# Spreading the output-weight splits of a paged-attention stage over more pages, and ordering three groups of casts

## The chip, the core and the metric

The kernel runs on one core of a Trainium2 chip. Its time is the device time of one execution, in microseconds (us). The profiled execution is one more execution, recorded by the hardware profiler.

## The reference

Two layers of a hybrid decoder: a Mamba-2 SSD layer and a multi-head latent attention (MLA) layer, on a prompt of 1024 tokens and on 8 samples of 8 new tokens with 2048 cached positions each. Everything is float32. The part of the reference that the change touches:

```python
def mla_prompt_attn(q_nope, q_pe, ckv, kpe, w_uk, w_uv):     # per block of 128 queries
    _, l, acc = latent_partial(absorb(qn, w_uk), qp, ckv, kpe, q_pos[:, None] >= k_pos[None, :])
    return latent_out(l, acc, w_uv)

def mla_sample_attn(q_nope, q_pe, ckv, kpe, pool_ckv, pool_kpe, layer, page_table, w_uk, w_uv):
    q_lat = absorb(q_nope, w_uk)
    stats = latent_partial(q_lat, q_pe, ckv, kpe, causal)          # the sample's own 8 keys
    def page_step(carry, pt):                                      # 16 pages of 128 keys
        page = latent_partial(q_lat, q_pe, pool_ckv[layer, pt], pool_kpe[layer, pt], None)
        return merge_partial(carry, page), None                    # running maximum, sum, values
    (_, l, acc), _ = lax.scan(page_step, stats, page_table.T)
    return latent_out(l, acc, w_uv)

def mla_output(o, gate, w_out):                                    # for prompt and samples
    gated = o.reshape(b, t, MLA_WIDTH) * jax.nn.silu(gate)
    return jnp.einsum('bte,ed->btd', gated, w_out)                 # 1024 x 1024
```

After that come the residual and a final RMSNorm.

## The kernel before

**Precision.** A float32 product is made as three matmuls on rounded operands: each operand is split into a high part and a low part (`hi` and `lo`), and hi·hi, hi·lo and lo·hi are summed. A split is two instructions: ScalarE (ACT) copies the source into `hi`, rounding it, and then VectorE (DVE) or GpSimd (POOL) subtracts: `lo = src - hi`. The helper `split` (lines 125 to 133) issues both; its argument `parts` cuts the subtraction into that many instructions.

**Stages.** The SSD layer ends at about 1060 us, the MLA projections at about 1335 us. Then come the prompt's sixteen heads (to about 1680 us), and the *pages stage* (from about 1680 us to about 1926 us), and a short tail.

**Heads.** `mla_heads` writes the order on TensorE (PE) and GpSimd by hand. Beside the attention of head h, units of preparation for head h+2 are merged in. For every fourth head `prep_group` (lines 1239 to 1271) loads the key weights (`wkr`, line 1245) and value weights, splits both, and makes eight value pieces (`vp`, written to `Vh` and `Vl`); the key weights (`w` in the trace) are used after the eighth piece, by `prep_kv`. The split of the key weights stands behind piece i = 3 in the text. The order of ACT, DVE and the DMA queue of SyncE (SP) is made by a planner that simulates the kernel: it may move an instruction ahead of the ones written before it, as soon as its inputs are there in the simulation. `issue_after(x)` restrains it: an instruction in that block that runs on x's own engine is placed behind x. On instructions of another engine it has no effect.

**Pages.** `Sample.flow` (lines 1777 to 1824) goes over 32 items, four for each sample, each of 4 x 128 keys; I call item n "page n". In the iteration n the hand-written PE order is: first half of the transposes of page n+1 (`turn(n+1, 0)`), transposes of the weights of page n-1 (`turn_p(n-1)`), the second half (`turn(n+1, 1)`), on every fourth page the transposes of a finished sample (`turn_acc`), scores of page n, a block of output matmuls (`next(out.fill)`), and values of page n-1. DVE and ACT make of that: `cTh`, `cTl` (turned page, high and low), `pTh`, `pTl` (turned weights), the maximum `mx` and its running negative `nm` (`softmax`, line 1635), the exponentials `P`, and the accumulator `ac`. GpSimd gathers page n+4 (`pgr`) and makes the low half `kvl` of page n+1 (`halves`).

**Output weights.** The eight blocks of 128 rows of `w_out`, in the order `WORD`, are split in the iterations that `WSP` lists: two each in pages 2, 3, 4 and 5. `weight_split` (lines 1867 to 1879) issues the copy `w5h` on ACT behind the turned page's `cTh` and four subtractions of 256 columns (`w5l`), on GpSimd for the first, third, fifth and seventh block, on DVE for the others (`WENG`), the latter behind `cTl`. Blocks 2 to 7 go through three load buffers (`w5r`) that the rows `h` of the output use later; the first two blocks have their own (`w5p`).

**Output rows.** `pieces` (lines 1881 to 1951) is a generator over eight tiles of 128 prompt rows. Its first step loads a tile (`og`), the second splits it (`oh` on ACT, `ol` as one DVE instruction of 1024 columns), and each further step issues 12 of a tile's 48 output matmuls (`p`). The flow takes the splitting step in page 5 (`OUT0[0] - 1`), one step in pages 6 and 7 (`OUT0`) and in every page after that, and a second one in pages 8 and 12 (`MORE`).

Of the kernel before, what the change touches and what calls it, by code (L numbers as in the profile page):

```python
# [8 lines left out]
F32 = mybir.dt.float32  # L9
F32R = mybir.dt.float32r  # L10
AF = mybir.ActivationFunctionType
ALU = mybir.AluOpType
# [25 lines left out]
SCALE = (NOPE + ROPE) ** -0.5  # L38
# [9 lines left out]
QG = 2  # L48
PRE = 4
Q0 = 9  # L50
OUT0 = (6, 7)
MORE = (8, 12)
WSP = (2, 2, 3, 3, 4, 4, 5, 5)
WENG = (2, 0, 2, 0, 2, 0, 2, 0)
WORD = (0, 4, 6, 1, 2, 3, 5, 7)
NWA = 8
# [26 lines left out]
def mm3(nc, out, pairs):  # L83
    n = len(pairs)
    for i, (a, b) in enumerate(pairs):
        nc.tensor.matmul(out, a, b, start=(i == 0), stop=(i == n - 1))  # L86
# [38 lines left out]
def split(k, hi, lo, src, eng=None, parts=0):  # L125
    nc = k.nc
    nc.scalar.copy(hi, src)  # L127
    n = parts and hi.shape[1] // parts
    for a in range(parts):
        s = slice(a * n, a * n + n)  # L130
        (eng or nc.vector).tensor_tensor(lo[:, s], src[:, s], hi[:, s].bitcast(F32), op=ALU.subtract)
    if not parts:
        return (eng or nc.vector).tensor_tensor(lo, src, hi.bitcast(F32), op=ALU.subtract)  # L133
# [1013 lines left out]
class Heads:  # L1147
# [91 lines left out]
    def prep_group(self, hg):  # L1239
        k, nc = self.k, self.k.nc  # L1240
        cs = slice(256 * hg, 256 * hg + 256)
        w8 = self.w8
        self.wkr = w8[0]
        self.wk = w8[2 + 2 * (hg % 2)], w8[3 + 2 * (hg % 2)]
        nc.sync.dma_start(self.wkr, self.wuk[:, cs].rearrange("(k p) e -> p k e", p=128))
        raw, wv = w8[1], w8[6:]
        nc.sync.dma_start(raw, self.wuv[:, cs].rearrange("(k p) e -> p k e", p=128))
        yield
        split(k, *wv, raw)
        if hg == 1:  # L1250
            self.ones_cols(1)
        yield
        vh, vl = self.V[hg % 2]
        for i in range(8):
            t0 = 128 * i
            p = self.wt(f"vp{hg}{i}")
            pairs = []
            for kk in range(2):
                a, b = k.kvh[:, kk, t0 : t0 + 128], k.kvl[:, kk, t0 : t0 + 128]
                pairs += [(a, wv[0][:, kk]), (a, wv[1][:, kk]), (b, wv[0][:, kk])]  # L1260
            mm3(nc, p[:, :256], pairs)
            src = p[:, :256].rearrange("p (a j v) -> p a j v", a=2, j=2)

            def dst(t):
                t = t[:, i]
                return bass.AP(t.tensor, t.offset, [list(t.ap[0]), [192, 2], [128, 2], [1, 64]])

            split(k, dst(vh), dst(vl), src)
            if i == 3:
                split(k, *self.wk, self.wkr)  # L1270
            yield

    def prep_kv(self, h):
# [265 lines left out]
class Sample:  # L1539
# [87 lines left out]
    def softmax(self, name, s, n, old):  # L1627
        nc = self.k.nc
        mx = self.small(name, "mx4", 1)
        nc.vector.reduce_max(mx, s, axis=AX.X)  # L1630
        nm = self.small(name, "nm4", 1, 4)
        if old is None:
            nc.vector.tensor_scalar(nm, mx, -SCALE, None, op0=ALU.mult)
        else:
            nc.vector.tensor_scalar(nm, mx, -SCALE, old, op0=ALU.mult, op1=ALU.min)
        P = self.sp.tile([128, n], F32, tag=f"P4{n}", name=f"P4{name}", bufs=2)
        l = self.small(name, "l4", 1, 4)
        nc.scalar.activation(P[:, :n], s, AF.Exp, bias=nm, scale=SCALE, accum_out=l)
        f = None
        if old is not None:  # L1640
            f = self.small(name, "f4", 1)
            nc.scalar.activation(f, old, AF.Exp, bias=nm, scale=-1.0)
        return nm, P, l, f
# [133 lines left out]
    def flow(self):  # L1777
        N = len(self.items)
        for n in range(-1, N + 1):
            t, out = n + 1 < N, self.out  # L1780
            if t:
                self.turn(n + 1, 0)
            if n % 4 == 1:
                self.first_acc(n // 4)
            if t:
                yield
            if n > 0:
                self.turn_p(n - 1)
            if t:
                self.turn(n + 1, 1)  # L1790
                yield
            if out:
                for x in range(WSP.count(n)):
                    out.weight_split(WORD[WSP.index(n) + x])
            if n % 4 == 1 and n > 4:
                self.turn_acc(n // 4 - 1)
            if 0 <= n < N:
                self.scores(n)
                self.weigh(n)
            if n % 4 == 3 and t:  # L1800
                self.first_scores(n // 4 + 1)
            if 0 <= n < N:
                yield
            if n % 4 == 0 and n < N:
                self.first_values(n // 4)
            if n >= 0 and n + PRE < N:
                self.load(n + PRE)
            if n == N - 2:
                self.late_loads()
            if n % 2 == 0 and n + 2 < N:  # L1810
                self.load_tk(n + 2)
            if out and (n in OUT0 or max(OUT0) < n <= N - HOLD):
                next(out.fill, None)
            if n > 0:
                self.values(n - 1)
            if t:
                self.halves(n + 1)
            if out:
                if n in MORE:
                    next(out.fill, None)  # L1820
                if n + 1 == OUT0[0]:
                    next(out.fill)
                    self.k.nc.sync.dma_start(out.fw, self.k.I["final_norm_w"].partition_broadcast(128))
            yield
# [27 lines left out]
class MlaOut:  # L1852
# [11 lines left out]
        self.raw[kk] = self.sp.tile([128, D], F32, tag="h5", name=f"w5r{kk}", bufs=3)  # L1864
        WQ(nc).dma_start(self.raw[kk], k.I["mla_w_out"][0][kk * 128 : kk * 128 + 128])

    def weight_split(self, kk):
        hi, lo = self.ws[kk]
        raw = self.raw.pop(kk)
        nc, x = self.k.nc, WENG[WORD.index(kk)]  # L1870
        with self.k.tc.issue_after(self.pins[0].ins):
            nc.scalar.copy(hi, raw)
        for a in range(4):
            s = slice(256 * a, 256 * a + 256)
            with self.k.tc.issue_after(self.pins[1].ins):
                (nc.gpsimd if x & 2 else nc.vector).tensor_tensor(lo[:, s], raw[:, s], hi[:, s].bitcast(F32),
                                                                  op=ALU.subtract)
        if 2 <= WORD.index(kk) < 5:
            self.weight(WORD[WORD.index(kk) + 3])

    def pieces(self, tiles, src=None):
        k, nc, sp, ws = self.k, self.k.nc, self.sp, self.ws

        def load(i):
            t0, m = TILES[i]
            oh = sp.tile([128, 8, 128], F32R, tag="oh5", name=f"oh5{i}", bufs=2)
            ol = sp.tile([128, 8, 128], F32R, tag="ol5", name=f"ol5{i}", bufs=2)
            g = src
            if i < 8:
                g = sp.tile([128, 8, 128], F32, tag="og5", name=f"og5{i}", bufs=2)  # L1890
                nc.sync.dma_start(g, k.og_d[:, :, t0 : t0 + m].rearrange("b p t -> p b t"))
            return oh[:, :, :m], oh[:, :, 64:] if m == 64 else ol, g, oh

        queue = [load(tiles[0])]
        if tiles[0] == 0:
            yield
        split(k, *queue[0][:3])
        if tiles[0] == 0:
            yield
        for n, i in enumerate(tiles):  # L1900
# [10 lines left out]
            for hf, c in enumerate(cs):  # L1911
                nw = c.stop - c.start
                tag = "tr" if src else "pj"
                p = self.psum.tile([128, 512], F32, tag=tag, name=f"p5{i}{hf}", bufs=SB[tag])
                for j, _ in enumerate(mm_tok(nc, p, m, nw, [
                        (oh[:, kk], ol[:, kk], o2[:, kk], ws[kk][0][:, c], ws[kk][1][:, c]) for kk in WORD])):
                    if j == (7 if src else 11) and nw == 512:
                        yield
                nc.vector.tensor_tensor(h[:m, c], h[:m, c], p[:m, :nw], op=ALU.add)
                if src:  # L1920
                    nc.vector.tensor_tensor(h[:m, c], h[:m, c], p[64:, :nw], op=ALU.add)
                    nc.scalar.activation(junk[:, c], h[:m, c], AF.Square, accum_out=ss[:m, hf : hf + 1])
                    if hf < 2:
                        nc.vector.tensor_tensor(h[:m, c], h[:m, c], self.fw[:m, c], op=ALU.mult)
                    if hf == 1:
                        nc.vector.tensor_tensor(ss[:m, 0:1], ss[:m, 0:1], ss[:m, 1:2], op=ALU.add)
                if hf == 0:
                    if n + 1 < len(tiles):
                        split(k, *queue[0][:3])
                if c.stop < D:  # L1930
                    yield
            if not src:
# [123 lines left out]
```

## Time and profile before

| | us |
|---|---|
| median of 3 runs | 1953.28 (1952.03 to 1955.74) |
| the profiled execution's own time | 1949.75 |
| its span, first to last instruction | 1948.0 |
| PE busy in the span | 1898.6 |
| DVE, ACT, POOL busy | 1189.8, 1108.4, 841.3 |

The profile is read from the page (totals, slices), then from views of the trace: busy time by stretch, waits by engine, and the instructions in order of time. In a row of the last kind stand the start, the time taken, the engine, the line in the kernel, the operation, output and input, and in brackets the idle time of that engine just before with what ended it.

### The profile page before, as it was taken

What the parts mean: (1) busy time and instruction counts of PE and PEld (TensorE: products, weight loads), DVE (VectorE), ACT (ScalarE), POOL (GpSimd) and SP (SyncE); (2) the same over time, 40 slices, a digit from 0 to 9 for tenths busy, and PEclk for the clock granted to TensorE, in tenths of its full rate; (3) what the DMA queues carried; (4) which work ended last, traced back from release to release, by engine and by line L of the source; (5) the groups of instructions that cost most, each with busy time, mean ns of one, the idle gap of its engine ahead of it and who ended that gap; (6) DMA issues with size and microseconds to landing.
All of it is one profiled execution on the core that took longest, in us unless ns stands there. A gap on an engine that the chain in (4) does not pass through costs nothing.

```text
span 1948.0 us, 33561 instructions
## 1 busy us (share of the span) xinstructions
PE 1898.6 (97%) x12023; PEld 1732.3 (89%) x12023; DVE 1189.8 (61%) x2423; ACT 1108.4 (57%) x2535; POOL 841.3 (43%) x1122
## 2 busy tenths in 40 slices
PE   9999999999999999899999999999999999899998
PEld 7999999999999999788788998898888888778887
DVE  5566565657666656755533104476787778666564
ACT  6466666667666666732214314336777777855552
POOL 2447455555655555443003212104443434865551
PEclk9999999999999999999999999999999999999999
DMA  5123223332323332544533333133111112654431
GB/s 167 48 72 93 86 85 97 84 108 84 96 81 96 86 95 82 190 161 156 181 114 117 123 150 94 56 109 94 48 49 41 51 40 59 215 181 149 144 128 38
DMA packets 181086, 202.01 MB, mean 104 GB/s; under 512 B 18828, under 2 KB 147608, under 8 KB 180536
## 3 DMA queue, kind: packets, MB, share of 16 engines
q1 hardware_dynamic: 175864, 180.08, 30.1%
q0 software_dynamic: 4976, 19.66, 2.9%
q8 instruction: 95, 1.56, 0.3%
q14 instruction: 71, 0.58, 0.1%
q10 hardware_dynamic: 80, 0.13, 0.0%
HBM read 146.52 MB, written 53.28 MB: 103 GB/s over the span
## 4 chain that ended last, share of the span: by engine, by line
PE 82%; ACT 5%; DMA 4%; DVE 4%; POOL 3%; issue 2%; SPq 0%; POOLq 0%; DVEq 0%; ACTq 0%
PE pj L86 19%; PE pz L98 8%; PE pq L98 6%; PE pob L98 5%; PE p L98 5%; PE poa L98 5%; PE sc L86 2%; PE py L635 2%; PE o L86 2%; DMA M<-acs_d 2%; PE o L1426 2%; PE sc L1363 2%; PE o L1428 2%; PE st L1395 2%; PE st L1397 2%
## 5 line engine op out<-in xcount | busy, mean ns | idle before, releaser
L86 PE MATMUL pj<-xh,wih 128*128 128x384 f32 (+1 forms) x768 | 254.2, 335 | 0.5 <-ACT raw L512 0.3
L86 PE MATMUL pj<-xl,wih 128*128 128x384 f32 (+1 forms) x768 | 253.7, 330 | 0.0
L86 PE MATMUL pj<-xh,wil 128*128 128x384 f32 (+1 forms) x768 | 253.2, 330 | 0.0
L1409 POOL TENSOR_TENSOR tl<-P,th 128x384 fp32r<-128x384 f32 (+1 forms) x96 | 91.3, 951 | 235.1 <-ACT P L1407 188.9
L526 DVE SCALAR_TENSOR_TENSOR acc<-raw,vec,acc 128x1112 f32<-128x1112 f32 x96 | 142.2, 1482 | 26.4 <-ACT acc L522 25.4
L86 PEld LDWEIGHTS pj<-xh,wih 128*128 128x128 f32 x768 | 143.9, 188 | 2.3 <-ACT xh L273 0.8
L86 PEld LDWEIGHTS pj<-xl,wih 128*128 128x128 f32 x768 | 144.5, 188 | 1.0
L86 PEld LDWEIGHTS pj<-xh,wil 128*128 128x128 f32 x768 | 144.4, 188 | 0.4
L98 PE MATMUL pz<-wih,xh 128*128 128x256 f32 x504 | 142.8, 287 | 0.6 <-ACT z L567 0.6
L98 PE MATMUL pz<-wil,xh 128*128 128x256 f32 (+1 forms) x504 | 140.2, 284 | 0.0
L1406 ACT ACTIVATE th<-st 128x512 fp32r<-128x512 f32 x192 | 94.5, 492 | 65.5 <-PE st L1402 50.5
L630 ACT ACTIVATE M<-M,tok 128x128 f32<-128x128 f32 (+1 forms) x288 | 90.9, 386 | 66.7 <-DVE M L627 66.3
L98 PE MATMUL pz<-wih,xl 128*128 128x256 f32 x448 | 128.3, 286 | 0.0
L1699 POOL TENSOR_TENSOR kvl<-pgr,kvh 128x256 fp32r<-128x256 f32 x128 | 96.3, 779 | 66.3 <-ACT kvh L1697 65.6
L98 PEld LDWEIGHTS pz<-wih,xh 128*128 128x128 f32 x504 | 95.9, 190 | 1.3 <-ACT z L567 1.0
L627 DVE TENSOR_TENSOR M<-M,negu 128x512 f32<-128x512 f32 x64 | 52.6, 822 | 68.3 <-DMA M<-acs_d 67.9
L1407 ACT ACTIVATE P<-st 128x512 f32<-128x512 f32 x192 | 93.7, 488 | 0.0
L98 PEld LDWEIGHTS pz<-wil,xh 128*128 128x128 f32 (+1 forms) x504 | 92.7, 184 | 0.7
L133 DVE TENSOR_TENSOR wil<-wraw,wih 128x512 fp32r<-128x512 f32 x88 | 71.3, 817 | 27.6 <-ACT wih L127 24.4
L613 POOL TENSOR_TENSOR xdd<-xsT,tok 128x256 f32<-128x256 f32 x64 | 50.8, 794 | 80.5 <-ACT xsT L599 80.1
L98 PEld LDWEIGHTS pz<-wih,xl 128*128 128x128 f32 x448 | 85.2, 190 | 0.1
L1409 DVE TENSOR_TENSOR tl<-P,th 128x512 fp32r<-128x512 f32 x96 | 70.9, 739 | 18.5 <-ACT P L1407 17.6
(832 smaller groups left out, 6302.7 us busy)
## 6 DMA issues: line engine op xcount, KB each, us to landing
wraw<-in_ssd_w_in SPq DMA_DIRECT2D x92, 256.0 KB
M<-acs_d SPq DMA_DIRECT2D x64, 256.0 KB
s<-in_state_ssm SPq DMA_DIRECT2D x32, 256.0 KB
y_d<-y SPq DMA_DIRECT2D x64, 128.0 KB
out_s_ssm<-s SPq DMA_DIRECT2D x32, 256.0 KB
wraw<-in_ssd_w_out SPq DMA_DIRECT2D x12, 512.0 KB
q_d<-qt SPq DMA_DIRECT2D x32, 192.0 KB
qp<-q_d SPq DMA_DIRECT2D x8, 768.0 KB
```

Source lines behind the costliest of these rows:

```text
L86: nc.tensor.matmul(out, a, b, start=(i == 0), stop=(i == n - 1))
L98: nc.tensor.matmul(o, a, b, start=(j == 0), stop=(j == len(ops) - 1))
L133: return (eng or nc.vector).tensor_tensor(lo, src, hi.bitcast(F32), op=ALU.subtract)
L526: last = nc.vector.scalar_tensor_tensor(acc, raw[:, j : j + n], k.convw[j][:, blk : blk + 1], acc, op0=ALU.mult, op1=ALU.add)
L613: nc.gpsimd.tensor_tensor(v3(xdd), v3(xsT), hb(2), op=ALU.mult)
L627: nc.vector.tensor_tensor(M[:m, :, :m], M[:m, :, :m], (k.negs if smp else k.negu)[:m, :m].unsqueeze(1).to_broadcast([m, 4, m]), op=ALU.add)
L630: nc.scalar.activation(M[:m, h, :m], M[:m, h, :m], AF.Exp, bias=tk[:, 0, 4 * g + h : 4 * g + h + 1])
L635: nc.tensor.matmul(py[:m, h * 64 : h * 64 + 64], M[:m, h, :m], xsT[:m, h * 64 : h * 64 + 64], start=True, stop=True)
L1406: nc.scalar.activation(th[:, :n], ps[:, :n], AF.Exp, scale=SCALE)
L1407: nc.scalar.activation(P[:, :n], ps[:, :n], AF.Exp, scale=SCALE)
L1409: eng.tensor_tensor(tl[:, :n], P[:, :n], th[:, :n].bitcast(F32), op=ALU.subtract)
L1699: nc.gpsimd.tensor_tensor(rl[:, j], raw[:, j], rh[:, j].bitcast(F32), op=ALU.subtract)
```

## The change

Four edits:

1. The eight blocks of the output weight are split in pages 2, 3, 4, 4, 5, 6, 6, 7. Each split is made in two halves: the copy and the first two subtractions are issued ahead of the page's scores (behind the turned page, as before), the other two behind the page's scores, and those on DVE behind the page's `nm`.
2. The steps of the output rows start two pages later (splitting in page 7, blocks in 8 and 9 and on), and the second steps are taken in pages 10, 12, 14 and 18. Their number up to page 32 is the same: 28 blocks.
3. `turn_acc` is issued behind the values of page n-1, no longer ahead of the scores. The subtraction `ol` of an output tile is made in four parts.
4. In `prep_group` the split of the key weights is placed behind the two instructions of the value piece i = 3.

```diff
-OUT0 = (6, 7)
-MORE = (8, 12)
-WSP = (2, 2, 3, 3, 4, 4, 5, 5)
+OUT0 = (8, 9)
+MORE = (10, 12, 14, 18)
+WSP = (2, 3, 4, 4, 5, 6, 6, 7)
@@ prep_group
-            split(k, dst(vh), dst(vl), src)
+            a = nc.scalar.copy(dst(vh), src)
+            b = nc.vector.tensor_tensor(dst(vl), src, dst(vh).bitcast(F32), op=ALU.subtract)
             if i == 3:
-                split(k, *self.wk, self.wkr)
+                with k.tc.issue_after(a.ins), k.tc.issue_after(b.ins):
+                    split(k, *self.wk, self.wkr)
@@ softmax
-            nc.vector.tensor_scalar(nm, mx, -SCALE, old, op0=ALU.mult, op1=ALU.min)
+            self.nmi = nc.vector.tensor_scalar(nm, mx, -SCALE, old, op0=ALU.mult, op1=ALU.min)
@@ flow
-            if out:
-                for x in range(WSP.count(n)):
-                    out.weight_split(WORD[WSP.index(n) + x])
-            if n % 4 == 1 and n > 4:
-                self.turn_acc(n // 4 - 1)
+            parts = [WORD[WSP.index(n) + x] for x in range(WSP.count(n))] if out else []
+            for kk in parts:
+                out.weight_split(kk, 0)
             if 0 <= n < N:
                 self.scores(n)
                 self.weigh(n)
+            if parts:
+                out.pins = out.pins[0], self.nmi
+            for kk in parts:
+                out.weight_split(kk, 1)
...
             if n > 0:
                 self.values(n - 1)
+            if n % 4 == 1 and n > 4:
+                self.turn_acc(n // 4 - 1)
@@ MlaOut
-    def weight_split(self, kk):
+    def weight_split(self, kk, half):
         hi, lo = self.ws[kk]
-        raw = self.raw.pop(kk)
+        raw = self.raw[kk]
         nc, x = self.k.nc, WENG[WORD.index(kk)]
-        with self.k.tc.issue_after(self.pins[0].ins):
-            nc.scalar.copy(hi, raw)
-        for a in range(4):
+        if not half:
+            with self.k.tc.issue_after(self.pins[0].ins):
+                nc.scalar.copy(hi, raw)
+        for a in range(2 * half, 2 * half + 2):
...
-        if 2 <= WORD.index(kk) < 5:
-            self.weight(WORD[WORD.index(kk) + 3])
+        if half:
+            del self.raw[kk]
+            if 2 <= WORD.index(kk) < 5:
+                self.weight(WORD[WORD.index(kk) + 3])
@@ pieces
-        split(k, *queue[0][:3])
+        split(k, *queue[0][:3], parts=4 if tiles[0] == 0 else 0)
...
-                        split(k, *queue[0][:3])
+                        split(k, *queue[0][:3], parts=4 if tiles[n + 1] < 8 else 0)
```

## The prediction, on record before the changed kernel was seen

> **What bounds the kernel now.** I read the totals first, then the waits of TensorE, then a table by stretch, then the instructions in order of time around the edits.
>
> ```profile
> PE 1898.6 (97%) x12023; PEld 1732.3 (89%) x12023; DVE 1189.8 (61%) x2423; ACT 1108.4 (57%) x2535; POOL 841.3 (43%) x1122
> PE 82%; ACT 5%; DMA 4%; DVE 4%; POOL 3%; issue 2%; SPq 0%; POOLq 0%; DVEq 0%; ACTq 0%
> ```
>
> PE is busy for 97% and carries 82% of the chain that ended last. The change removes no matmul, so it can only win where PE waits or runs slowly.
>
> ```profile
> PE o L86 <- DVE pTl L133: 5.4, 3, 2.4
> PE act L1757 <- DVE ac L1750: 2.7, 1, 2.7
> PE pt L1726 <- ACT P L1638: 0.9, 2, 0.5
> PE o L86 <- ACT pTh L127: 0.6, 1, 0.6
> 1682.00:1690.00 8.00, 6.88 (x45) 5.84 (x43) 5.71 (x10) 6.12 (x13) 5.33 (x7) 1.00 0.53 178
> 1690.00:1698.00 8.00, 5.57 (x30) 5.16 (x29) 8.00 (x18) 7.08 (x14) 7.81 (x10) 0.79 1.05 343
> 1698.00:1706.00 8.00, 4.49 (x30) 3.36 (x28) 7.49 (x9) 6.38 (x12) 7.81 (x10) 1.00 1.06 321
> 1706.00:1714.00 8.00, 5.71 (x25) 4.64 (x25) 7.45 (x14) 1.61 (x2) 7.72 (x10) 0.79 0.81 244
> 1714.00:1722.00 8.00, 7.74 (x49) 6.93 (x50) 4.89 (x12) 5.42 (x12) 4.91 (x6) 1.00 0.81 264
> 1722.00:1730.00 8.00, 8.00 (x53) 7.18 (x52) 4.56 (x12) 4.58 (x12) 3.85 (x5) 1.00 0.53 186
> ```
>
> The first four rows are PE's waits from 1681 to 1722 us (total, times, longest): 9.6 us. The others give busy time of PE, weight load, DVE, ACT and POOL in stretches of 8 us, then the granted clock. The five stretches to 1722 have 9.6 us of idle PE too, while DVE and POOL are full from 1690 to 1714; after 1722 PE is full. Twice the granted clock is 0.79: 2 x 0.21 x 8 = 3.4 us of work lost. So the split pages lose 13.0 us, and that is the ceiling of edits 1 and 3.
>
> What fills DVE there, in order of time:
>
> ```profile
> 1687.74 2.94 DVE L1876 TENSOR_TENSOR w5l<-w5p,w5h 128x256 fp32r<-128x256 f32 x4 [1.62 <-ACT w5h L1872]
> 1692.61 0.39 PE L86 MATMUL o<-kvh,pTl 128*128 128x256 f32 x1 [2.43 <-DVE pTl L133]
> 1701.17 4.64 DVE L133 TENSOR_TENSOR ol<-og,oh 128x1024 fp32r<-128x1024 f32 x1
> 1718.25 1.42 DVE L1876 TENSOR_TENSOR w5l<-w5r,w5h 128x256 fp32r<-128x256 f32 x4
> L1876 DVE TENSOR_TENSOR w5l<-w5r,w5h x12: 406/844/953, 1693.3 to 1719.2; 128x256 fp32r<-128x256 f32 x12
> L1876 POOL TENSOR_TENSOR w5l<-w5r,w5h x12: 716/813/1748, 1694.3 to 1713.2; 128x256 fp32r<-128x256 f32 x12
> ```
>
> A block's four subtractions stand ahead of the maximum and of `pTl`, and PE, which needs `pTl`, waits 2.43 us; a 1024-wide `ol` of 4.64 us stands ahead of `ac`, and `turn_acc` waits for that in front of the scores (the 2.7 us of the second wait row). A part on DVE takes 406 ns at best and 844 ns at the median; the four at 1718.25 took 1.42 us and those at 1687.74, beside POOL's own, 2.94.
>
> The last place is in the heads:
>
> ```profile
> 1446.80 0.62 ACT L127 CAST w<-w 128x512 fp32r<-128x512 f32 x1 [2.15 <-DMA w<-in_mla_w_uk]
> 1447.94 0.50 PE L1395 MATMUL st<-qTh,kTh 98*128 98x512 f32 x1 [1.49 <-ACT P L1407]
> 1535.94 0.62 ACT L127 CAST w<-w 128x512 fp32r<-128x512 f32 x1 [2.63 <-DMA w<-in_mla_w_uk]
> 1537.09 0.50 PE L1395 MATMUL st<-qTh,kTh 98*128 98x512 f32 x1 [1.95 <-ACT P L1407]
> L86 PE MATMUL vp<-w,kvh x28: 277/282/333, 1462.5 to 1473.5; 128*128 128x256 f32 x28
> ```
>
> The planner put the key weights' cast on ACT as soon as it believed their DMA landed; the chip's ACT waits 2.15 and 2.63 us for it, with the attention's exponentials behind it, and PE stands still for 1.49 and 1.95 us.
>
> **The change, part by part.**
>
> *Key weights (edit 4).* The cast moves behind piece 3 of the group. The pieces of the group loaded at 1442 run from 1462.5 us on (last row), 15 us after the early cast, so the DMA has landed. Removed: 1.49 + 1.95 = 3.4 us. Moved: 0.62 us on ACT and one subtraction on DVE, into a stage where PE is the bound; the cover is the two score tiles of lead, and if it is gone the cost is at most those 0.62 us twice, 1.2. I take 0: **-3.4**, bounds -3.4 and -2.2. Queued behind the pinned cast are the exponentials, as before, but without a wait in front.
>
> *Pages (edits 1 to 3).* I compare from the scores of page 2 to those of page 8:
>
> ```profile
> 1681.20 0.48 PE L86 MATMUL sc<-cTh,qlh 128*128 128x512 f32 x1
> 1686.54 0.48 PE L86 MATMUL sc<-cTh,qlh 128*128 128x512 f32 x1
> 1700.59 0.39 PE L86 MATMUL o<-kvh,pTl 128*128 128x256 f32 x1 [1.64 <-DVE pTl L133]
> 1707.11 0.78 PE L86 MATMUL sc<-cTh,qlh 128*128 128x512 f32 x1
> 1716.83 0.40 PE L98 MATMUL p<-w5h,oh 128*128 128x512 f32 x1
> 1719.58 0.28 PE L86 MATMUL o<-kvh,pTh 128*128 128x256 f32 x1
> 1730.07 0.48 PE L86 MATMUL sc<-cTh,qlh 128*128 128x512 f32 x1
> ```
>
> Now that is 1730.07 - 1681.20 = 48.9 us. It holds two output blocks of 2.75 us (1719.58 - 1716.83), in pages 6 and 7, that the change moves to pages 10 to 18, where PE is full and each costs its 2.75 us again. So these six pages must take under 48.9 - 5.5 = 43.4 us to win. PE's own work in them is 43.4 - 13.0 = 30.4, or 5.07 a page.
>
> What each page takes after the change:
> - Pages 2 and 5 have one block, on POOL. DVE has its ordinary work (the first four of these rows, over six pages): two `cTl`, `pTl`, the maximum, `nm`, `ac` and `ln`:
>
> ```profile
> L1688 DVE TENSOR_TENSOR cTl<-ct,cTh 128x512 fp32r<-128x512 f32 x12 | 8.2, 682 | 2.7 <-ACT cTh L1687 2.7
> L1630 DVE TENSOR_REDUCE mx<-sc 128x1 f32<-128x512 f32 x6 | 4.1, 681 | 0.5 <-PE sc L86 0.5
> L133 DVE TENSOR_TENSOR pTl<-pt,pTh 128x512 fp32r<-128x512 f32 x6 | 4.1, 680 | 0.0
> L1747 DVE SCALAR_TENSOR_TENSOR ac<-ac,f,o 128x256 f32<-128x256 f32 x6 | 2.9, 477 | 2.2 <-PE o L86 2.1
> L1699 POOL TENSOR_TENSOR kvl<-pgr,kvh 128x256 fp32r<-128x256 f32 x23 | 16.9, 763 | 3.2 <-ACT kvh L1697 2.8 <-issue 0.3
> L1619 POOL DMA_INDIRECT pgr<-in_cache_ckv,ptidx x6 | 6.3, 1042 | 1.5 <-POOL kvl L1699 0.9 <-POOL w5l L1876 0.5 <-DMA w5r<-in_mla_w_out 0.2
> L133 DVE TENSOR_TENSOR ol<-og,oh x8: 1210/1226/4641, 1696.9 to 1886.3; 128x1024 fp32r<-128x1024 f32 x8
> ```
>
>   (8.2 + 4.1 + 4.1 + 2.9)/6 = 3.2 us, and some 0.5 for `nm` and `ln` (an estimate from the smaller groups): 3.7. PE bounds these pages: 5.07 plus the wait for `P`, 0.5 (third wait row): 5.6.
> - Pages 3 and 7 have one block on DVE, pages 4 and 6 one on DVE and one on POOL. DVE then has 3.7 + 0.4 of small things + four parts: 3.0 beside a POOL split (the 2.94 row), 1.6 alone (4 x 406), so 7.1 in pages 4 and 6 and from 5.7 to 7.1 in pages 3 and 7, where POOL is busy for half the page; the middle is 6.4. The halves now stand behind `nm`, so the maximum no longer waits for four.
> - `ol` of the first tile, four parts of 256 columns, adds 1.6 to 3.4 us. DVE has 5.6 - 3.7 = 1.9 free in each of pages 2 and 5, and the planner fills gaps; I add 1.0.
>
> Sum: 2 x 5.6 + 2 x 7.1 + 2 x 6.4 + 1.0 = 39.2, against 43.4: **-4.2**. Bounds: all parts alone, 2 x 5.6 + 4 x 5.7 = 34.0, -9.4; all beside POOL and `ol` not hidden, 2 x 5.6 + 4 x 7.1 + 3.4 = 43.0, -0.4. No single wait in this is near 2.4 us, so I let the clock stay at 1.00, as after the 1.64 us wait at 1700.59 (the next stretch at 0.79 follows the wait for `ac`); that is inside the sum.
>
> POOL's own load is 4 blocks x 4 parts x 0.81 = 13 us, and six times (4 x 0.76 for `kvl` + 1.04 for the gather) = 24.5: 37.5 us in 39.2, nearly full but one page of slack ahead of PE. The second half of a POOL block isn't held by `nm`, which is on another engine; only its page changes. `turn_acc` behind the values costs nothing: it waits for `ac` of a page before, and its 0.4 us of PE work stays.
>
> The row that speaks against the DVE parts is 406/844/953: the same subtraction at twice the time. The Trainium skill, "GPSIMD Engine Reference", section "1. Specifications", says that GpSimd shares its SBUF interfaces with VectorE and that instructions with two SBUF inputs contend. By that rule alone every part pays while POOL runs, which is the upper bound above. The trace agrees as far as it goes: `w5l` and `ol`, with two such inputs, are stretched, `cTl` and `pTl`, which read PSUM, stay at 680 ns.
>
> *Later pages.* The double pages 12 and 18 begin a new half tile right behind a finished one, which waits for the addition of the finished one (page 12 and 18 by the count of blocks; before, page 12 alone):
>
> ```profile
> PE p L98 <- DVE h L1919: 0.6, 1, 0.6
> ```
>
> One more such wait: **+0.6**, from 0 to 0.6. The casts and subtractions of `ol` in four parts cost 8 x (4 x 0.41 - 1.22) = 3 us of DVE in all, against a free DVE (3.4 of 8 us in the stretch at 1722); PE hides it, and in a page without slack it would cost 0.4.
>
> **Sum.** -3.4 - 4.2 + 0.6 = -7.0 us. The profiled execution took 1949.75 us, 1.75 above its span; that would become 1942.8. It lies 3.5 us below the median, 1953.28, to which I apply the same difference: **1946.3 us**.
>
> **The rivals.**
> 1. *Slower: the split pages stay bound by DVE and POOL.* Pages 3 and 4 lasted from 1686.54 to 1707.11 (scores to scores), 10.3 us each, with both engines full. If pages 4 and 6, with two blocks, take 10.3 again (the planner, which doesn't know the slow parts, packs them ahead of `pTl`) and the four others 7.5, the six take 50.6: 7.2 over 43.4. With -3.4 and +0.6: +4.4, **1957.7**. It decides from 8.3 us a page on. For it: DVE at 8.00 of 8. Against it: the work is spread over six pages, and the chain scores, maximum, exponential gets ahead of half of it. 12%.
> 2. *The heads gain, the pages don't*: the work returns as smaller waits for `pTl`, `P` and `kvl`; 43.0 instead of 39.2, so -3.4 - 0.4 + 0.6 = -3.2: **1950.1**. It includes the case that the planner had these orders anyway. 12%.
> 3. *SP becomes the wait.* SP issues in order, and the late rows stand in front of the keys:
>
> ```profile
> 1711.98 8.08 SPq L1904 DMA_DIRECT2D h<-h_d  x3
> 1724.07 0.32 SPq L1612 DMA_DIRECT2D tk<-kpe_dh  x1
> ```
>
>    The three `h` loads take 8.08 us of queue, since their buffers come free with the last `w5l`. The last blocks are split later now; if those loads stand ahead of `tk` of page 8, its scores start late by about half a page, 3.5 us: -3.5, **1949.8**. Against it: today `tk` is issued at 1724.07, 6 us ahead of the scores of page 8. 10%.
> 4. *PE's floor is reached*: 34.0 and no second wait: -12.8, **1940.5**. 6%.
>
> **How the numbers follow.** My forecast has 60%, and its own bounds go from -3.4 - 9.4 to -2.2 - 0.4 + 0.6. The range holds rivals 2, 3 and 4 and half of rival 1: 1940.5 to 1955.0. A measurement of this kernel can tell about 0.2%, 3.9 us, from no change. Faster by more: the forecast but for its weak end, and rival 4: 0.66. Within: rivals 2 and 3 and that end: 0.22. Slower: rival 1: 0.12.
>
> **What would show it.** In the profile after: no ACT wait on `in_mla_w_uk` of 2 us and no PE wait on `P` at those heads; the waits on `pTl` and `ac` in the split pages under 3 us together, and the stretches' clock at 1.00; scores of page 2 to page 8 in about 39 us; the `w5l` parts on DVE still between 0.4 and 0.9 us; a second wait on `h`. I am wrong if those six pages take over 43 us, if PE waits for `kvl` or `tk`, or if the stretches after them aren't full.

## The result and the profile after

| | before | after |
|---|---|---|
| median of 11 runs each | 1951.14 us | 1946.67 us |
| ratio, 95% interval | | 0.9969 (0.9959 to 0.998): -6.0 us |
| profiled execution, its own time (span) | 1949.75 (1948.0) | 1942.63 (1940.9) |

The ratio is worked out from all the runs; the two medians alone lie 4.5 us apart. The total came out where it was forecast, for reasons that were only partly the forecast ones. That 1946.67 is so near the forecast 1946.3 is partly luck: the forecast was counted from 1953.28 us, and beside the kernel after the kernel before took 1951.14. First the page after, with the same two lines as before:

```profile
PE 1896.4 (98%) x12023; PEld 1731.9 (89%) x12023; DVE 1191.3 (61%) x2447; ACT 1110.6 (57%) x2535; POOL 844.3 (44%) x1122
PE 85%; ACT 4%; DVE 3%; DMA 3%; POOL 2%; issue 1%; SPq 0%; POOLq 0%; DVEq 0%; ACTq 0%
```

Such totals hardly move. Next, PE's waits in the heads (1335 to 1660 us; total, times, longest), before and then after:

```profile
PE st L1395 <- ACT P L1407: 3.9, 3, 1.9
```

```profile
PE st L1397 <- ACT P L1409: 0.4, 1, 0.4
```

The two stalls of 1.49 and 1.95 us behind the key weights' cast are gone; the third wait of the row, 0.4 us, is there in both. Now the waits of the split pages after (1668 to 1745 us), and the table by stretch:

```profile
PE pt L1728 <- ACT P L1640: 3.5, 4, 1.9
PE pt41n L1667 <- ACT P41n L1640: 3.2, 1, 3.2
PE o L86 <- DVE pTl L133: 1.7, 2, 1.0
```

```profile
1682.00:1690.00 8.00, 5.88 (x41) 4.93 (x39) 7.49 (x16) 5.88 (x12) 7.08 (x9) 1.00 1.05 364
1690.00:1698.00 8.00, 5.91 (x24) 4.93 (x25) 8.00 (x15) 6.83 (x13) 4.94 (x6) 0.55 1.02 279
1698.00:1706.00 8.00, 7.06 (x39) 6.05 (x38) 6.98 (x14) 4.08 (x8) 7.82 (x12) 0.81 0.72 240
1706.00:1714.00 8.00, 6.11 (x38) 5.12 (x37) 7.55 (x14) 7.28 (x13) 7.81 (x11) 1.00 0.74 227
1714.00:1722.00 8.00, 7.01 (x48) 6.05 (x47) 7.05 (x17) 4.39 (x11) 7.19 (x9) 1.00 0.80 258
```

The waits for `pTl` and `ac` shrank as forecast, but 3.2 us in front of the exponential of a sample's new keys (`P41n`) and 3.5 us for `P` came in their place, 8.4 us in all, and the clock fell further: (0.45 + 0.19) x 8 = 5.1 us of work lost. Waits and clock together are 13.5 us; before they were 13.0. In the order of time, page 3 shows the new wait being made:

```profile
1685.11 3.86 DVE L1883 TENSOR_TENSOR w5l<-w5p,w5h 128x256 fp32r<-128x256 f32 x4
1687.84 1.05 ACT L127 CAST oh<-og 128x1024 fp32r<-128x1024 f32 x1 [0.82 <-DMA og<-og_d]
1689.74 2.00 ACT L1879 CAST w5h<-w5r 128x1024 fp32r<-128x1024 f32 x2
1692.09 0.38 PE L1667 MATMUL pt41n<-ident,P41n 128*8 128x128 f32 x1 [3.25 <-ACT P41n L1640]
```

DVE's four subtractions are not two and two here: all four stand ahead of the new keys' maximum. A cast `oh` of the output rows, which the text places four pages later, and two casts `w5h` stand on ACT ahead of the new keys' exponential.

### The profile page after: what moved, and what is told of

The parts are those of the page before. It is cut to its first block, busy times and chain, and to the rows that moved or that the text cites. A ratio compares the mean times of both kernels' runs of the same rounds, so it can differ in the third digit from the quotient of the medians.

```text
span 1940.9 us, 33581 instructions
## 1 busy us (share of the span) xinstructions
PE 1896.4 (98%) x12023; PEld 1731.9 (89%) x12023; DVE 1191.3 (61%) x2447; ACT 1110.6 (57%) x2535; POOL 844.3 (44%) x1122
## 4 chain that ended last, share of the span: by engine, by line
PE 85%; ACT 4%; DVE 3%; DMA 3%; POOL 2%; issue 1%; SPq 0%; POOLq 0%; DVEq 0%; ACTq 0%
PE pj L86 21%; PE pz L98 8%; PE pq L98 6%; PE pob L98 5%; PE p L98 5%; PE poa L98 5%; PE py L635 2%; PE sc L86 2%; PE o L86 2%; PE sc L1365 2%; PE o L1428 2%; PE o L1430 2%; PE st L1397 2%; PE st L1398 2%; PE st L1399 2%; PE o L1429 2%
```

## Where the time went, stage by stage

Every trace of this study can be cut at the same instructions: A, from the first head's matmul `qs<-ident,qp` (at 1277.6 us in before, while the projections still run) to page 2's matmul `sc<-tk`; B, from there to the same matmul of page 8, less 5.5 us for the two output blocks where pages 6 and 7 hold them; C, from page 8's to page 31's, less the same 5.5 us where those blocks are there instead. The fifth column is the busy time of DVE's sixteen subtractions `w5l`, two rounded rows added; the last is (1 - granted clock) x time from 1674 to 1738 us. All are worked out from start times and rows like those quoted; the kernels are told of below.

| trace | A | B | C | `w5l` on DVE | clock loss |
|---|---|---|---|---|---|
| before | 405.1 | 43.4 | 179.5 | 10.7 | 3.4 |
| before_again | 404.1 | 43.8 | 179.5 | 12.9 | 5.1 |
| key_only | 400.8 | 46.8 | 179.5 | 16.8 | 6.8 |
| acc_only | 404.7 | 47.7 | 178.1 | 16.8 | 6.8 |
| key_acc | 400.5 | 43.8 | 178.1 | 13.2 | 5.1 |
| after | 400.6 | 43.4 | 178.3 | 13.6 | 5.1 |
| after_again | 400.7 | 46.4 | 178.3 | 11.3 | 6.8 |
| no_key | 404.3 | 45.3 | 178.3 | 12.1 | 6.8 |
| new_keys | 401.6 | 47.0 | 178.3 | 11.7 | 8.5 |
| rows_pinned | 400.7 | 43.9 | 178.4 | 14.0 | 1.7 |
| no_pool_split | 400.5 | 39.7 | 178.3 | 7.6 | 1.7 |

A and C repeat to within about 1 us and each falls into two groups, by edit 4 and by the place of `turn_acc`. B does not repeat: it spreads over 3 us and more for one and the same order of instructions (before and key_only, after and after_again). Its spread is waiting and clock, not work: B less PE's idle time, and less half of the time in which PE was busy at half clock, is 29.9 to 31.0 us in all eleven traces.

## The experiments

**key_only: edit 4 alone.** The kernel before with the key weights' split inside `issue_after` of both instructions of the value piece, as in the change.

> The kernel before with edit 4 alone (the split of the key weights behind the value piece). Theory (the heads carry nearly all the gain): the three PE waits on P in the heads (3.9 us in all) go, the heads from the marker at 1277.6 us to 1619.5 us get shorter by about 4.4 us, the pages from the scores of page 2 to those of page 8 stay at 48.9 us, and the time falls by about 4.5 us (ratio 0.9977). Rival (the recorded prediction's split): 3.4 us in the heads, so ratio 0.9983, and the rest in the pages. Second rival (the planner had a free choice and the gain came from elsewhere): no change.

Measured: ratio 0.9986 (0.997 to 1.0001), -2.7 us. The time alone is not decisive; the trace is: A is 400.8, and the waits on `P` in the heads are the one row of 0.4 us that the kernel after has (two of the three went, not all). Over ten traces with edit 4 and four without it (the three kernels further down included), A is 400.8 and 404.5 on the mean: **3.7 us**.

The surprise is B, 3.4 us longer than before, although each engine's instructions in the pages stand in the same order as before. DVE and GpSimd in page 5 of this trace:

```profile
1700.75 7.22 DVE L1878 TENSOR_TENSOR w5l<-w5r,w5h 128x256 fp32r<-128x256 f32 x4
1707.89 0.68 DVE L133 TENSOR_TENSOR pTl<-pt,pTh 128x512 fp32r<-128x512 f32 x1
```

```profile
1701.51 2.77 POOL L1701 TENSOR_TENSOR kvl<-pgr,kvh 128x256 fp32r<-128x256 f32 x4
1704.25 2.76 POOL L1878 TENSOR_TENSOR w5l<-w5r,w5h 128x256 fp32r<-128x256 f32 x4
1707.16 1.04 POOL L1621 DMA_INDIRECT pgr<-in_cache_ckv,ptidx  x1 [0.15 <-POOL w5l L1878]
```

and the durations of the same subtractions, min/median/max in ns, from 1700 to 1709 us:

```profile
L1878 DVE TENSOR_TENSOR w5l<-w5r,w5h x4: 411/420/6203, 1700.7 to 1707.6; 128x256 fp32r<-128x256 f32 x4
```

One subtraction of 411 ns took 6203: it stood still while GpSimd ran eight subtractions back to back, and `pTl` and PE (6.5 us, its longest wait) stood behind it.

**no_key: the change without edit 4.** The inverse edit.

> The kernel after without edit 4. Theory (heads carry the gain, the six pages gain nothing, the later pages about 1.2 us): heads as before with three waits on P of 3.9 us, the six pages 43.4 us without output blocks, time 1.2 us below the kernel before (ratio 0.9994). Rival (the pages carry what the recorded prediction gave them): 3.6 to 4.2 us below (ratio 0.998).

Measured: 0.9981 (0.9965 to 0.9998), -3.7 us; A 404.3, B 45.3, C 178.3. The interval holds both -1.2 and -4.2, so the time does not tell the theories apart. The stages do: A is back at the level of before, B is no better than in the traces with before's splits, and C keeps its gain. The waits on `P` in the heads came back as two of 1.9 us in all, not three of 3.9; the rest of A is clock, as told under before_again.

**acc_only: `turn_acc` behind the values, alone.**

```diff
-            if n % 4 == 1 and n > 4:
-                self.turn_acc(n // 4 - 1)
             if 0 <= n < N:
...
                 self.values(n - 1)
+            if n % 4 == 1 and n > 4:
+                self.turn_acc(n // 4 - 1)
```

> The kernel before with one part of edit 3 alone: the transposes of the finished accumulator behind the values, no longer ahead of the scores. Theory: the weight load's wait on the accumulator (1.3 us in five of the later samples) goes, each later sample gets shorter by about 0.2 us, 1.2 in all; the wait of 2.7 us in page 5 goes too, but as the chain of page 5 (the 4.64 us subtraction of the output row) stays ahead of the next wait, it comes back in part as a wait on P or on the turned weights; in all 1.2 to 3.5 us less (ratio 0.9994 to 0.998). Rival (the recorded prediction's sentence that the move costs and brings nothing): no change in the later pages, and 2.7 us in page 5 at most.

Measured: 0.9984 (0.997 to 0.9998), -3.1 us. C is 178.1 against 179.5: **1.3 to 1.4 us**, and this row of before, the weight load's waits from 1740 to 1900 us, has no counterpart any more:

```profile
PEld act L1757 <- ACT ac L1676: 1.3, 5, 0.4
```

The wait of 2.7 us in page 5 is not there either, but it is absent from key_only and before_again too, where `turn_acc` stands as before, so the move need not be its cause. B did not profit: 47.7, with a wait of 7.4 us on `pTl` of the same kind as in key_only.

**new_keys: the new keys' maximum and exponential ahead of the second half.**

```diff
+            if n % 4 == 3 and t:
+                self.first_scores(n // 4 + 1)
             if parts:
-                out.pins = out.pins[0], self.nmi
+                out.pins = out.pins[0], self.nmi if n % 4 < 3 else self.nmn
...
-            if n % 4 == 3 and t:
-                self.first_scores(n // 4 + 1)
@@ weight_split
-            with self.k.tc.issue_after(self.pins[0].ins):
+            with self.k.tc.issue_after(self.pins[0].ins), self.k.tc.issue_after(self.sm.newe.ins):
                 nc.scalar.copy(hi, raw)
```

Here `nmn` is the new keys' negative maximum and `newe` their exponential.

> The kernel after, with the work for a sample's own new keys (their scores, maximum and exponential, which follow every fourth page) ahead of the second half of the weight split, on DVE and on ACT too. Theory (the six pages gained nothing because in page 3 four subtractions on DVE and three casts on ACT stand ahead of the new keys' maximum and exponential): the wait of 3.2 us on the new keys' exponential goes, the stretch behind it at half clock (0.55 over 8 us, 3.6 us of work) runs at 1.00, and the six pages get shorter by 3 to 7 us than after's 43.4. Rival (DVE and GpSimd are the bound of these pages, whatever their order): the wait returns on the turned weights or on P in page 4, and the six pages stay within 1 us of 43.4.

Measured: 0.9985 (0.9973 to 0.9997), -2.9 us. The wait on the new keys fell from 3.2 to 0.8 us, as meant, and the pages did not get shorter: 47.0 us, outside both expectations, with 2.3 us on `pTl`, 2.1 on `P`, and the largest clock loss of all, 8.5. My theory, that the order around the new keys is what ate the gain, fell.

**key_acc: everything but the spreading.** The edits of key_only and acc_only together, measured on the same chip as the next run.

> The kernel before with edit 4 and the transposes of the finished accumulator behind the values: all of the change but the spreading of the splits over six pages. Theory (the spread brings nothing on the mean): 3.9 us less in the heads and 1.4 us less in the later pages, so 5.3 us below the kernel before (ratio 0.9973), and within 1 us of the kernel after that runs beside it. Rival (the spread brings 2 to 4 us on the mean, and the one pair of traces hid it): 2 to 4 us above the kernel after.

**after_again: the kernel after, a second trace.**

> The kernel after once more, for a second trace and a comparison on the same chip. Theory (the time of the subtractions beside GpSimd differs from execution to execution): the heads and the later pages repeat to 0.3 us (400.6 us from the first head's marker to the scores of page 2, 183.75 us from page 8 to page 31), the six pages differ by 1 to 4 us from the 43.4 us of the first trace, and so do the total times of the subtractions on DVE. Rival (the order sets the time): the six pages repeat to 0.3 us as well.

Measured: key_acc 1948.77 us, ratio 0.9977 (0.9966 to 0.9988), -4.5 us; after_again 1949.93 us, 0.9974 (0.996 to 0.9989), -5.1 us. The kernel without the spreading is 1.2 us below the one with it, by medians of twelve runs each: as fast, to within what this can tell, and not the 2 to 4 us slower of the rival. And the same program repeats A and C to 0.1 us, while B goes from 43.4 to 46.4. This time DVE was hardly delayed, and GpSimd was:

```profile
1698.52 1.42 DVE L1883 TENSOR_TENSOR w5l<-w5r,w5h 128x256 fp32r<-128x256 f32 x4
1699.86 1.42 DVE L131 TENSOR_TENSOR ol<-og,oh 128x256 fp32r<-128x256 f32 x4
```

```profile
1698.45 5.63 POOL L1701 TENSOR_TENSOR kvl<-pgr,kvh 128x256 fp32r<-128x256 f32 x4 [3.90 <-ACT kvh L1699]
1714.00 1.03 POOL L1621 DMA_INDIRECT pgr<-in_cache_ckv,ptidx  x1 [0.16 <-POOL w5l L1883]
```

```profile
1715.33 1.09 PE L1686 MATMUL ct<-ident,pgr 128*128 128x128 f32 x4 [3.00 <-DMA pgr<-in_cache_ckv,ptidx]
```

While DVE ran eight subtractions in 2.7 us, one `kvl` on GpSimd took 3.4 us (four took 5.63; they take 2.8 elsewhere). GpSimd's later work came late, gathers included, and PE waited 3.00 us for a gathered page. Not all of that is GpSimd's: this gather, issued at 1707.0 us, also took longer to land than its counterpart of the first trace, issued at 1700.0, where 5.9 us passed:

```profile
DMA to landing us min/median/max: 8.2/8.2/8.2
```

Why it took longer stays open.

**no_pool_split: GpSimd's subtractions left out.** Its four low halves are set to zero once, ahead of the pages.

> The kernel after without GpSimd's sixteen subtractions of the output weight: it leaves out the low halves of four blocks, which are zero. Theory (DVE's subtractions are stretched by GpSimd's): the sixteen on DVE fall from 13.6 us in all to between 6.5 (0.41 each) and 9.6 (0.6 each), and the six pages from 43.4 to between 36 and 39 us. Rival (they are stretched by the gathers and the low halves of the keys, which stay): 12 us or more in all, and the six pages at 42 or more.

Measured in one trace: the sixteen on DVE take 7.6 us, against 13.6 and 11.3 in the kernel after, B is 39.7 against 43.4 and 46.4, the clock loss is 1.7. The first number is in the theory's range, the second 0.7 us above it.

```profile
L1888 DVE TENSOR_TENSOR w5l<-w5r,w5h 128x256 fp32r<-128x256 f32 x12 | 4.9, 457 | 0.0
L1888 DVE TENSOR_TENSOR w5l<-w5p,w5h 128x256 fp32r<-128x256 f32 x4 | 2.7, 741 | 0.0
```

**before_again: the kernel before, a second trace.**

> The kernel before once more, for a second trace of the same program. Theory (the split pages differ from execution to execution, the rest repeats): 405 us from the first head's marker to the scores of page 2 and 179.5 us from page 8 to page 31 to within 0.8 us, and pages 2 to 8 at 47 to 53 us, with DVE's twelve later parts between 7.8 and 14 us. Rival (the 48.9 us of the first trace are the kernel's own): 48.9 to within 0.5 us.

Measured: A 404.1, C 179.5; from page 2 to page 8 49.3 us (B 43.8), and the twelve later parts 10.0 us against 7.8. This pair alone lies within the rival's 0.5 us; that the spread is there is shown by key_only (46.8 in the same order) and by the two traces of the kernel after.

A holds a surprise. Of the two stalls in the heads only the first is there; the cast of 1535.94 in before waits 0.38 us here instead of 2.63, and PE does not wait behind it. But behind the first stall the clock fell to half, with PE busy (the second row has the columns of the table by stretch, the clock third from the end):

```profile
PE st L1395 <- ACT P L1407: 2.0, 2, 1.5
```

```profile
1455.87:1459.28 3.41, 3.41 (x10) 2.73 (x9) 2.85 (x6) 2.98 (x6) 1.51 (x2) 0.50 0.00 2
```

That costs 3.41 / 2 = 1.7 us. acc_only and no_key show the same: one stall of 1.8 and 1.5 us, 3.41 us at half clock, no second stall. None of the ten traces with edit 4 has either.

The last four kernels look for something better. For these the pages 2 to 10 are compared, without output blocks: the kernel after takes 53.2 and 56.1 us, no_key 55.0.

**rows_pinned: the output rows' splits held back.**

```diff
...
+        with self.behind(not src):
             split(k, *queue[0][:3], parts=4 if tiles[0] == 0 else 0)
...
```

`behind` opens `issue_after` blocks: for the first tile on page 5's turned page and `nm`. The later tiles' splits are in the same way held behind the `nm` of the page in which they are written.

> The kernel after with the splits of the output rows held back: the first tile's behind page 5's turned page and nm, the others behind the nm at which they are written; in the kernel after the planner had moved eight to twelve of these subtractions (4.6 to 6.7 us of DVE) and two casts into pages 3 and 4. Theory (DVE's load in pages 3 and 4, which the planner adds to, holds the scores and the new keys' exponential up): the wait in front of the new keys stays, but pages 4 and 5 get shorter, and pages 2 to 8 take 40 to 43 us against 43.4, 45.3 and 46.4 in the three traces of after's order. Rival (a subtraction moved is a subtraction done, and the stretch beside GpSimd follows it to page 5 and 6): 43 to 47 us.

Measured: 0.9961 (0.9948 to 0.9975), -7.6 us; B 43.9, in the rival's range; pages 2 to 10 take 53.8. The waits grew to 11.1 us and the clock loss shrank to 1.7. Whether it is faster than the kernel after stays open: the intervals overlap.

**eight_pages: one block a page.**

```diff
-OUT0 = (8, 9)
-MORE = (10, 12, 14, 18)
-WSP = (2, 3, 4, 4, 5, 6, 6, 7)
+OUT0 = (10, 11)
+MORE = (12, 14, 16, 18, 20, 22)
+WSP = (2, 3, 4, 5, 6, 7, 8, 9)
```

> The kernel after with one block of the output weight a page, in pages 2 to 9, DVE's and GpSimd's in turn, and the output rows two pages later again (second steps in pages 12, 14, 16, 18, 20 and 22). In the first trace of the kernel after, pages 2 to 9 take 53.2 us without their two output blocks (43.4 + 7.95 + 7.27 - 5.5). Theory (a page with splits on both engines is what DVE and GpSimd can't do in 5.1 us): four pages of 5.6 and four of 5.7 to 7.1 us, 48 us in all, 5 us less (ratio to the kernel before 0.994). Rival (the subtractions are stretched by GpSimd's other work as much, and each page with a DVE block takes 8 us whatever the engine of its neighbours): 53 us or more, no gain.

Measured: 0.9965 (0.9952 to 0.9978), -6.8 us; pages 2 to 10 take 53.3 us, the rival's number, against 53.2 and 56.1. The 5 us of the theory are not there; whether it is a little faster than the kernel after stays open, since the intervals overlap.

**eight_all and eight_all_dve: all of it, and then the engine.** The edits of new_keys, rows_pinned (behind page 8) and eight_pages together; then only `WENG` from (2, 0, 2, 0, 2, 0, 2, 0) to eight zeros, which puts all blocks on DVE.

> One block a page in pages 2 to 9, with the new keys' maximum and exponential ahead of the second half of the split, and with the splits of the output rows held back behind page 8. On DVE no group of four subtractions is left: two stand ahead of nm and two behind it. In the earlier trace of one block a page the pages 2 to 10 took 53.3 us; the three of after's order 53.2, 55.0 and 56.1 (without two output blocks). Theory (order and spreading are both needed: then no wait is long enough for the clock to fall): no wait over 2 us, granted clock 1.00 in every stretch from 1682 to 1730 us, and pages 2 to 10 in 47 to 50 us; 4 us below one block a page alone, 6 us below the kernel after (ratio to the kernel before 0.9945). Rival (the stretch of DVE's subtractions beside GpSimd makes new waits wherever they stand): 53 us or more and a clock loss of 3 us or more; the ratio stays at 0.9965.

> The same with all eight blocks on DVE and none on GpSimd. Theory (GpSimd's subtractions are what stretches DVE's): 32 parts at 0.46 to 0.55 us instead of 0.7 to 0.85, GpSimd has time for its gathers, DVE has 4.1 + 1.9 = 6.0 us a page, pages 2 to 10 take 48 to 50 us: the same as with both engines or up to 2 us more. Rival (the keys' low halves and the gathers stretch them as much): 32 parts at 0.75 or more, 7.1 us a page, 57 us.

Measured: eight_all 0.9959 (0.9945 to 0.9972), -8.0 us; pages 2 to 10 in 51.5 us, between theory and rival; no wait over 2.0 us, and the granted clock 1.00 throughout the pages, as the theory said. eight_all_dve **0.9948 (0.9933 to 0.9963), -10.2 us, 1943.65 us**: the lowest of all here and below the kernel before. Against the kernel after (0.9974, 0.996 to 0.9989, on another chip) the intervals still touch, and against eight_all by much more, so there the traces speak: its pages 2 to 10 take 47.4 us, 4.1 less than eight_all's, where the expectation was the same or up to 2 us more. Durations of its subtractions, and PE's waits in the pages:

```profile
L1887 DVE TENSOR_TENSOR w5l<-w5r,w5h x24: 410/414/874, 1695.7 to 1726.2; 128x256 fp32r<-128x256 f32 x24
L1887 DVE TENSOR_TENSOR w5l<-w5p,w5h x8: 416/419/427, 1685.9 to 1691.9; 128x256 fp32r<-128x256 f32 x8
```

```profile
PE pt L1730 <- ACT P L1640: 2.6, 3, 1.4
PE o L86 <- DVE pTl L133: 2.4, 3, 1.3
PE pt L1730 <- issue: 0.4, 1, 0.4
```

Twice the number of subtractions on DVE cost 12.8 us, hardly more than half of them did before (11.3 in eight_all), since nearly every one now takes 0.41 us. GpSimd's `kvl` and gathers are still there, so it was GpSimd's own splits that made the collisions frequent (one trace of each kernel).

## Why the prediction was right in the sum and wrong in its parts

- **Heads, -3.4: right in cause and size, by luck in its second term.** Measured 3.7 in the stages; the two stalls went (before's row: 3.9 us, after's: 0.4). But the 1.95 us is a stall of one execution: the three other traces without edit 4 have only the first one, and 1.7 us of clock behind it, a cost that the prediction did not have and that happens to be about as large. The moved cast cost nothing that shows, as taken.
- **Pages, -4.2: wrong.** The step that failed is the price of DVE's parts, 3.0 for four beside a GpSimd split and 1.6 alone, added up to a page time. In five traces with before's splits (two of them with `turn_acc` moved) B is 43.4, 43.8, 46.8, 47.7 and 43.8, in three of after's 43.4, 46.4 and 45.3: means of 45.1 and 45.0. The spreading by itself was worth about nothing, which key_acc confirms in its time. The 16 parts took 11.3 to 13.6 us where I counted 2 x 3.0 + 2 x 2.3 = 10.6, and no mean price describes them: one part can cost 0.41 or 6.2. By the prediction's own sign of being wrong, six pages over 43 us, this part failed. My break-even from one trace, 43.4, was itself the lowest of the five, and the 4.64 us `ol` with its wait of 2.7 us, which I read as the order's, is in that trace alone.
- **"The maximum no longer waits for four", and `ol` at 1.0 us: wrong in pages 3 and 4.** The planner kept four parts together in both; in page 3 the new keys' maximum stands behind them. And it pulled the output rows' `oh` and `ol` in from four pages later: eight parts of `ol`, two tiles, ran there in 1.41 and 3.56 us, not one tile in the free time of pages 2 and 5. But undoing that (new_keys, rows_pinned) did not shorten B, so it isn't the cause by itself.
- **The clock stays at 1.00: wrong.** The table's loss is 5.1 and 6.8 us in the two traces of the kernel after, 4.5 and 6.1 of it while PE was busy.
- **GpSimd "one page of slack ahead of PE": wrong in some executions.** after_again waited 3.00 us for a gather, no_key 2.52.
- **Later pages, +0.6: wrong in sign.** Measured -1.3. The wait on `h` that I priced is not in a double page: it lies behind the last page's scores in both kernels (at 1923.7 us before, 1916.6 after), and no second one came. And I gave `turn_acc` behind the values no gain, though five weight loads of later samples waited for `ac`.
- **Sum.** -3.7 - 0.1 - 1.3 = -5.1 us by stages; the two comparisons give -6.0 (-8.0 to -3.9) and -5.1 (-7.8 to -2.2). The forecast of -7.0 lay in both because two errors, 4.1 too much in the pages and 1.9 too little behind them, partly cancelled. Of the rivals, the second (the heads gain, the pages don't) describes the mechanism best; its price, -3.2, lacked the later pages.

What is shown and what is not: that DVE's and GpSimd's subtractions hold each other up is shown by no_pool_split and by eight_all_dve against eight_all. That this is the whole of B's spread is argued from the rows, not shown: B does not follow DVE's busy time in the three traces of after's order, and in after_again a gather's slower landing had its part.

## What to carry to other kernels

Before trusting a stage's time from one trace, take a second trace of the same program: here the disputed stage of the kernel after moved by 3 us with nothing changed, most of the 4.2 that were forecast for it, while the stages around it repeated to 0.1 us; and a stall of 1.95 us in the heads of the kernel before was gone in its second trace. When two engines hold each other up, spreading the same collisions over more pages moves little; giving the contested kind of work to one engine, even to the busier one, removed nearly all of them. And a mean duration with a maximum far above it (406/844/953, 1210/1226/4641) is a queue to be explained, not a price to be multiplied.

## What the runs showed of the hardware

**The two engines block each other for whole instructions.** A DVE subtraction with both inputs in SBUF takes 0.41 us alone and typically 0.95 when GpSimd's are interleaved with it, but it took 6.2 in key_only, when GpSimd ran eight in a row; in after_again it was GpSimd that took 3.4 us for one of 0.7. `cTl`, `pTl` and `mx`, which read PSUM, stayed at 0.66 to 0.69 in the pages of all traces. The Trainium skill, "SBUF — State Buffer", section "Who interferes with whom", says that the pair of ports that the two engines share is an exclusive lock, and that a DVE instruction with two SBUF inputs contends with a GpSimd instruction that reads SBUF; that the loser is blocked fully and not throttled it says of DVE's two-port modes. The trace agrees with the full block here too: 6203 ns is no stretched 411. What decides who wins no run here shows; the same program came out both ways.

**The half clock comes in pieces of 3.4 us, and a piece counts, not a wait.** The clock losses of the table are multiples of about 1.7 us, which is 3.4 us at half clock. The shortest and the longest, one from no_pool_split and one from the kernel after (columns as above, the clock third from the end):

```profile
1690.00:1691.00 1.00, 1.00 (x7) 1.00 (x8) 1.00 (x3) 0.79 (x3) 1.00 (x3) 0.88 1.01 410
1691.00:1694.00 3.00, 3.00 (x16) 3.00 (x16) 3.00 (x9) 1.13 (x3) 2.73 (x4) 0.50 1.09 356
1694.00:1695.00 1.00, 1.00 (x6) 0.87 (x6) 1.00 (x5) 1.00 (x2) 0.27 (x1) 0.91 1.05 397
```

```profile
1689.00:1691.00 2.00, 0.00 (x0) 0.00 (x0) 2.00 (x9) 2.00 (x4) 0.54 (x1) 0.96 1.04 377
1691.00:1692.00 1.00, 0.00 (x0) 0.00 (x0) 1.00 (x3) 1.00 (x4) 0.00 (x0) 0.50 1.18 316
1692.00:1701.00 9.00, 8.91 (x33) 7.45 (x34) 9.00 (x15) 6.94 (x13) 7.79 (x9) 0.50 0.80 229
1701.00:1702.00 1.00, 0.83 (x5) 0.54 (x3) 1.00 (x3) 0.00 (x0) 0.97 (x3) 0.96 0.45 133
```

The first is 0.24 + 3.00 + 0.18 = 3.4 us, the second 10.2. The Trainium skill, "TensorE: Matmul & The Clock Gate", part 1, tells of free-running windows of about 3.4 us, where an idle one lowers the clock and a busy one restores it. The lengths agree. A single wait doesn't tell what follows: the short piece followed a wait of only 0.96 us, while waits of 1.96 us in eight_all were followed by none. What tells more is PE's busy time in the whole piece before. Here are one piece of before, ahead of a half clock, and the two of eight_all over which its 1.96 us are spread:

```profile
1689.70:1693.12 3.42, 0.99 (x6) 0.79 (x7) 3.42 (x9) 2.65 (x4) 3.23 (x5) 1.00 1.09 367
```

```profile
1703.28:1706.70 3.42, 2.13 (x18) 1.87 (x16) 3.42 (x6) 0.84 (x2) 3.39 (x5) 1.00 0.89 271
1706.70:1710.11 3.41, 2.74 (x17) 2.43 (x17) 2.86 (x7) 3.41 (x8) 3.01 (x5) 1.00 0.89 266
```

All fourteen traces, cut from 1674 us on into twenty such pieces each, in step with their half clocks, give for the pieces at full clock:

| PE busy in the piece | pieces | half clock in the next |
|---|---|---|
| 1.47 us or less | 17 | 17 |
| 1.74 to 2.49 us | 39 | 5 |
| 2.50 us or more | 188 | 0 |

So "idle" here doesn't mean without work. Nor is "busy" PE's own column: in the kernel after it was busy for 8.91 of 9.00 us and stayed at half clock all the while. Of the 36 pieces at half clock, the 14 with weight loads busy for 2.54 us or less were followed by another, the 22 with 2.74 us or more by full clock. These are counts from the rows; no run tests them. For the pages it means that a wait costs its own length, and 1.7 us or more on top where the waits of one piece add up.
